# One backbone step: the first MLP product by seven products of blocks in place of eight

## The chip, the core and the metric

One Trainium2 chip, one core. A core has a matrix engine (TensorE, PE in the profile; PEld is its loading of weights), a vector engine (VectorE, DVE), a scalar engine (ScalarE, ACT), GpSimd (POOL), and SyncE (SP), whose queue issues nearly all DMA transfers here. Each runs its instructions in their written order and waits on semaphores for the others. Sixteen DMA engines move data between DRAM and on-chip memory. The metric is device time of one execution, in microseconds (us).

## What is computed

One inference step of a layer on 640 tokens (512 of a sample, 128 of a prompt) of width D = 1024: modulated normalisation, four token mixers (pooling, Fourier, RWKV-7, gated linear attention), a gated merge, an output product and a residual; then the part that is changed:

```
h  = rmsnorm(xf) * (1 + scale) + shift
ff = square(relu(h @ mlp_w1)) @ mlp_w2      # w1: 1024 x 4096, w2: 4096 x 1024
xf = xf + g2 * ff                           # then a last rmsnorm
```

All of it is fp32. TensorE's fast form (`fp32r`) keeps fewer bits, so each fp32 operand is split into a high part (a cast) and a low part (what the cast lost), and a product is three matmuls: high x high, low x high, high x low.

## The kernel before

It is recorded in Python through tile pools; a scheduler sets each engine's order, and work under `hi()` goes ahead of other work. Weights come through one helper: `fetch` (L241) has SP load a tile of 128 x 512 (256 KB) into one of three raw buffers `wr`; `split` has ACT cast it to the high part (L246) and DVE subtract for the low part (L247), after which the raw buffer is free.

Before the MLP, the output product (L1247) runs tile by tile of 128 tokens. For each tile, `projected` (L1307 to L1309) adds the residual to `xf` on DVE and has ACT sum the squares, `normed` makes the reciprocal root on DVE (`rs`, L1313 to L1316), and `transposed` has PE transpose the tile (L1332), ACT apply scale and shift into `tm` (L1336) and cast to `nh` (L1338), DVE subtract for `nl` (L1339). The last tile (i = 4) is transposed within the MLP's first group.

The MLP has four groups of 8 feature tiles of 128 (32 tiles make 4096). In a group the first product comes first: `hidden` (L1361) runs 24 matmuls (8 steps of 128 along D, three terms) for a feature tile and one half of the tokens (HN = 320), then ACT and DVE make relu squared and split it into `fh` and `fl` (L1365 to L1368). The second product (L1407, 512 columns wide) sums the 8 feature tiles into five PSUM banks for each half of the output columns, and `residual` (L1395, L1396) multiplies by g2 and adds to `xf`. The last half of the last group stands apart (L1427), so that each tile of tokens can be finished and stored.

In the RWKV scan, earlier on, `new_x` has POOL copy inputs of a step (L854), twice per step.

Of the kernel before, what the change touches and what calls it, by code (L numbers as in the profile page):

```python
# [19 lines left out]
P = 128  # L20
# [116 lines left out]
def backbone(ctx, tc, a, y_prompt, y_sample, out_rwkv, out_gla):  # L137
# [482 lines left out]
        finish()  # L620
    pf_.close()

    def split_into(y, j, src):
        S.copy(y[0][:, j, :], src)
        V.tensor_tensor(y[1][:, j, :], src, f32(y[0][:, j, :]), ALU.subtract)
# [60 lines left out]
    for hp in range(2):  # L686
# [161 lines left out]
        def new_x(step):  # L848

            x = upool.tile([P, 4, 2, 2, 64], F32, name="xc", tag="xc", bufs=3)  # L850
            for smp in (True, False)[: 2 if step < 2 else 1]:
                ch = slice(0, 2) if smp else slice(2, 4)
                for O_, par in ((HR[0], 1), (HR[1], 0)):
                    (S.copy if step == 0 else G.tensor_copy)(x[O_, ch, par], pick(VT, step, smp)[O_].unsqueeze(2).broadcast_to([64, 2, 2, 64]))  # L854
            return x

        x = new_x(0)
# [425 lines left out]
    nh = h2.tile([P, KT, NT], F32R, name="nh")  # L1283
    nl = h2.tile([P, KT, NT], F32R, name="nl")
    pf1 = ctx.enter_context(tc.tile_pool(name="pf1", bufs=3, space=PSUM, reuse_waits="tile"))
    ops = ExitStack()
    op = ops.enter_context(tc.tile_pool(name="opool", bufs=1, side="right", reuse_waits="tile"))

# [12 lines left out]
    def projected(i, hf, acc, t):  # L1301
        c = i // 4
        if c not in g1b:
            g1b[c] = h2.tile([P, D], F32, name="g1b", tag="g1b")
# [4 lines left out]
        S.activation(t[:, bs], xf[i][:, bs], AF.Square, accum_out=ss[:, 2 * i + hf : 2 * i + hf + 1])  # L1309

    def normed(i, t):
        with hi():
# [6 lines left out]
    def project(i, hfs, t):  # L1319
        for hf in hfs:  # L1320
# [2 lines left out]
                out_terms(acc, i, k, hf)  # L1323
            projected(i, hf, acc, t)

    def transposed(i, t):
        c = i // 4
        sl_ = slice(i * P, i * P + P)
        for k4 in range(2):
            pt = pbank()  # L1330
            for k in range(4):
                PE.transpose(pt[:, k * P : k * P + P], t[:, (k4 * 4 + k) * P : (k4 * 4 + k) * P + P], ident)  # L1332
            tm = op.tile([P, 4, P], F32, name="tm", tag="tm", bufs=2)
            for k in range(4):
                kk = k4 * 4 + k
                S.activation(tm[:, k], pt[:, k * P : k * P + P], AF.Identity, scale=s2[:, kk, c : c + 1], bias=b2[:, kk, c : c + 1])  # L1336
            ks = slice(k4 * 4, k4 * 4 + 4)
            S.copy(nh[:, ks, sl_], tm)  # L1338
            V.tensor_tensor(nl[:, ks, sl_], tm, f32(nh[:, ks, sl_]), ALU.subtract)  # L1339

    for i in range(4):
        projected(i, 0, accs[i], ot())
# [10 lines left out]

    with tc.tile_pool(name="mlp", bufs=1, reuse_waits="tile") as mp, \
            tc.tile_pool(name="pf2", bufs=5, space=PSUM, reuse_waits="tile") as pf2:
        def hidden(w, h, l, b):
            pt = pbank()
            bs = slice(b * HN, b * HN + HN)
            for k in range(KT):
                for n, (wk, m) in enumerate(((w[0], nh), (w[0], nl), (w[1], nh))):  # L1360
                    PE.matmul(pt[:, :HN], lhsT=wk[:, k, :], rhs=m[:, k, bs], start=k == 0 and n == 0,  # L1361
                              stop=k == KT - 1 and n == 2)
            with hi():
                rl = mp.tile([P, HN], F32, name="rl", tag="rl", bufs=3)
                S.activation(rl, pt[:, :HN], AF.Relu)  # L1365
                V.tensor_tensor(rl, rl, pt[:, :HN], ALU.mult)  # L1366
                S.copy(h[:, bs], rl)
                V.tensor_tensor(l[:, bs], rl, f32(h[:, bs]), ALU.subtract)  # L1368

        g2b = mp.tile([P, 2, D], F32, name="g2b")  # L1370
        gf = mp.tile([P, D], F32, name="gf")
        NG = 4
        for g in range(NG):
            ws, fh, fl = [], [], []
            order = [(f, b) for f in range(8) for b in range(2)]
            if g == 0:
                order[:4] = [(0, 0), (1, 0), (0, 1), (1, 1)]
            for f, b in order:
                if b == 0:
                    ws.append(load(a["t_w1"][g * 8 + f]))  # L1380
                    fh.append(mp.tile([P, NT], F32R, name="fh", tag="fh", bufs=11))
                    fl.append(mp.tile([P, NT], F32R, name="fl", tag="fl", bufs=11))
                elif f == 0 and g == 0:
                    with hi():
                        transposed(4, before)
                    ops.close()
                hidden(ws[f], fh[f], fl[f], b)
            if g == 0:
                for cnd in range(2):
                    nc.sync.dma_start(out=g2b[:, cnd, :], in_=grow[1][cnd : cnd + 1, :].broadcast_to([P, D]))  # L1390
                nc.sync.dma_start(out=gf, in_=a["final_g"].rearrange("(o d) -> o d", o=1).broadcast_to([P, D]))
            def residual(i, hf, acc):
                cs_ = slice(hf * 512, hf * 512 + 512)
                t = mp.tile([P, 512], F32, name="mt", tag="mt", bufs=3)
                V.tensor_tensor(t, g2b[:, i // 4, cs_], acc, ALU.mult)  # L1395
                V.tensor_tensor(xf[i][:, cs_], xf[i][:, cs_], t, ALU.add)  # L1396

            for hf in range(2 if g < NG - 1 else 1):
                acc = [pf2.tile([P, 512], F32, name="pf2", tag="pf2") for _ in range(5)]
                for k2 in range(4):  # L1400
                    wh, wl = load(a["t_w2"][g * 4 + k2, hf])
                    for kk in range(2):
                        k = k2 * 2 + kk
                        for i in range(5):
# [6 lines left out]
                        residual(i, hf, acc[i])  # L1411


        h2pool.close()
        with tc.tile_pool(name="w2pool", bufs=1, side="right", reuse_waits="tile") as w2p:
# [54 lines left out]
```

## Time and profile before

| what | value |
|---|---|
| median of 3 runs | 1220.24 us (1218.92 to 1222.08) |
| profiled execution | 1224.66 us, its span 1222.9 us |
| granted clock, mean | 0.988 |
| PE busy | 1176.4 us (96%) |
| DVE busy | 733.5 us (60%) |
| ACT busy | 506.7 us (41%) |
| POOL busy | 62.3 us (5%) |
| chain that ended last | PE 77%, DVE 8%, DMA 7%, ACT 4% |

The span goes from the first to the last instruction of the profiled execution; the rest of its time lies around it. The chain is followed back from the last instruction, each step to what released it. Rows of windows read: stretch in us, its length, then busy us and instructions (x) of PE, PEld, DVE, ACT and POOL, then the granted clock of PE as a share of full speed (1.00 is 2.4 GHz), the share of the DMA engines' time, and GB/s. In rows of a timeline the bracket tells how long the engine stood before, and what ended that.

### The profile page before, as it was taken

What the parts mean: (1) busy time and instruction counts of PE and PEld (TensorE: products, weight loads), DVE (VectorE), ACT (ScalarE), POOL (GpSimd) and SP (SyncE); (2) the same over time, 40 slices, a digit from 0 to 9 for tenths busy, and PEclk for the clock granted to TensorE, in tenths of its full rate; (3) what the DMA queues carried; (4) which work ended last, traced back from release to release, by engine and by line L of the source; (5) the groups of instructions that cost most, each with busy time, mean ns of one, the idle gap of its engine ahead of it and who ended that gap; (6) DMA issues with size and microseconds to landing.
All of it is one profiled execution on the core that took longest, in us unless ns stands there. A gap on an engine that the chain in (4) does not pass through costs nothing.

```text
span 1222.9 us, 19633 instructions
## 1 busy us (share of the span) xinstructions
PE 1176.4 (96%) x7556; PEld 1017.1 (83%) x7556; DVE 733.5 (60%) x1458; ACT 506.7 (41%) x1028; POOL 62.3 (5%) x98
## 2 busy tenths in 40 slices
PE   7999999899999999997999989999999999999996
PEld 2778998789778898795588978998899899889985
DVE  4797785675588583447987757543443354245456
ACT  4732225742376522378635325532143123213332
POOL 0000000500114200300000000000000000000000
PEclk9999898999999999999999999999999999999999
DMA  9558661334314343056624560322222222222222
GB/s 357 205 173 251 201 224 57 104 93 119 101 36 122 103 148 95 30 170 212 195 93 141 179 208 18 99 75 69 77 79 85 71 79 78 70 87 69 78 87 86
DMA packets 85971, 147.41 MB, mean 121 GB/s; under 512 B 21693, under 2 KB 26206, under 8 KB 85878
## 3 DMA queue, kind: packets, MB, share of 16 engines
q1 hardware_dynamic: 85878, 146.16, 37.8%
q8 instruction: 59, 0.97, 0.3%
q14 instruction: 34, 0.28, 0.1%
HBM read 123.17 MB, written 22.95 MB: 119 GB/s over the span
## 4 chain that ended last, share of the span: by engine, by line
PE 77%; DVE 8%; DMA 7%; ACT 4%; issue 3%; SPq 0%; POOL 0%; DVEq 0%; ACTq 0%; POOLq 0%
PE pt L368 23%; PE pf L1361 18%; PE pf L1407 16%; PE po L1247 3%; PE pf L1427 2%; PE px L1084 2%; DMA araw<-in_t_ada_dram 2%; PE px L499 2%; DVE acc L309 2%; DVE wl L247 1%; PE px L287 1%; DMA wr<-in_t_in_dram 1%; DMA wr<-in_t_out_dram 1%; DMA wr<-in_t_w_dram 1%; PE px L775 1%
## 5 line engine op out<-in xcount | busy, mean ns | idle before, releaser
L246 ACT CAST wh<-wr 128x512 fp32r<-128x512 f32 x222 | 133.4, 618 | 349.5 <-PE pf L1407 139.1
L247 DVE TENSOR_TENSOR wl<-wr,wh 128x512 fp32r<-128x512 f32 x222 | 152.2, 700 | 206.9 <-ACT wh L246 202.4
L368 PE MATMUL pt<-xl,wh 128*128 128x320 f32 x816 | 200.5, 321 | 0.0
L368 PE MATMUL pt<-xh,wh 128*128 128x320 f32 x816 | 199.7, 321 | 0.0
L368 PE MATMUL pt<-xh,wl 128*128 128x320 f32 x816 | 196.1, 318 | 0.0
L1361 PE MATMUL pf<-nh,wl 128*128 128x320 f32 x512 | 158.1, 309 | 0.0
L1361 PE MATMUL pf<-nl,wh 128*128 128x320 f32 x512 | 158.0, 309 | 0.0
L1361 PE MATMUL pf<-nh,wh 128*128 128x320 f32 x512 | 157.9, 309 | 0.0
L368 PEld LDWEIGHTS pt<-xh,wh 128*128 128x128 f32 x816 | 138.9, 191 | 8.8 <-issue 4.1
L368 PEld LDWEIGHTS pt<-xl,wh 128*128 128x128 f32 x816 | 139.5, 191 | 6.8 <-issue 3.0
L368 PEld LDWEIGHTS pt<-xh,wl 128*128 128x128 f32 x816 | 138.9, 191 | 4.9 <-issue 1.7
L1407 PE MATMUL pf<-wl,fh 128*128 128x512 f32 x280 | 109.0, 389 | 0.0
L1407 PE MATMUL pf<-wh,fh 128*128 128x512 f32 x280 | 109.0, 389 | 0.0
L1407 PE MATMUL pf<-wh,fl 128*128 128x512 f32 x280 | 108.9, 389 | 0.0
L1361 PEld LDWEIGHTS pf<-nl,wh 128*128 128x128 f32 x512 | 96.0, 187 | 0.2
L1361 PEld LDWEIGHTS pf<-nh,wh 128*128 128x128 f32 x512 | 96.0, 188 | 0.1
L1361 PEld LDWEIGHTS pf<-nh,wl 128*128 128x128 f32 x512 | 96.0, 187 | 0.0
L309 DVE SCALAR_TENSOR_TENSOR acc<-araw,sc,acc 128x512 f32<-128x512 f32 x112 | 78.4, 746 | 11.9 <-DMA araw<-in_t_ada_dram 11.9
L1407 PEld LDWEIGHTS pf<-wh,fl 128*128 128x128 f32 x280 | 52.6, 188 | 11.0
L1407 PEld LDWEIGHTS pf<-wh,fh 128*128 128x128 f32 x280 | 52.6, 188 | 10.9
L1407 PEld LDWEIGHTS pf<-wl,fh 128*128 128x128 f32 x280 | 52.6, 188 | 10.7
L1366 DVE TENSOR_TENSOR rl<-rl,pf 128x320 f32<-128x320 f32 x64 | 31.0, 484 | 39.0 <-ACT rl L1365 39.0
(540 smaller groups left out, 1754.2 us busy)
## 6 DMA issues: line engine op xcount, KB each, us to landing
wr<-in_t_w_dram SPq DMA_DIRECT2D x128, 256.0 KB, 3.0
wr<-in_t_in_dram SPq DMA_DIRECT2D x102, 256.0 KB, 3.5
araw<-in_t_ada_dram SPq DMA_DIRECT2D x64, 256.0 KB, 3.5
adaw<-in_t_ada_dram SPq DMA_DIRECT2D x16, 512.0 KB, 9.2
mscr<-gate SPq DMA_DIRECT2D x24, 320.0 KB, 4.3
mg<-mscr SPq DMA_DIRECT2D x24, 320.0 KB, 3.8
uscr<-mg SPq DMA_DIRECT2D x15, 320.0 KB, 2.8
wr<-in_t_branch_dram SPq DMA_DIRECT2D x32, 128.0 KB, 2.1
```

What stands on the lines that cost most here:

```text
L246: S.copy(wh, raw)
L247: V.tensor_tensor(wl, raw, f32(wh), ALU.subtract)
L287: PE.matmul(pt[0:8, :], lhsT=c[:, 4 * part : 4 * part + 8, k + j], rhs=w[:, j], start=part == 1 and k + j == 0 and n == 0, stop=part == 0 ...
L309: V.scalar_tensor_tensor(acc[j], raw, w, acc[j], ALU.mult, ALU.add)
L368: PE.matmul(pt[:, b, :HN], lhsT=w, rhs=m[:, b * HN : b * HN + HN], start=start and n == 0, stop=stop and n == 2)
L499: PE.matmul(pt[:, :HN], lhsT=lhsT, rhs=rhs[:, b * HN : b * HN + HN], start=True, stop=True)
L1084: PE.matmul(pt, lhsT=ek[:, ts_], rhs=em[:, :, ts_], start=True, stop=True)
L1247: PE.matmul(acc, lhsT=m[k][:, sl_], rhs=W[k, hf][w][:, 0, :], start=k == 0 and n == 0, stop=k == KT - 1 and n == 2)
L1361: PE.matmul(pt[:, :HN], lhsT=wk[:, k, :], rhs=m[:, k, bs], start=k == 0 and n == 0, stop=k == KT - 1 and n == 2)
L1366: V.tensor_tensor(rl, rl, pt[:, :HN], ALU.mult)
L1407: PE.matmul(acc[i], lhsT=m[k][:, ts_], rhs=w[:, kk, :], start=k == 0 and n == 0, stop=k == 7 and n == 2)
L1427: PE.matmul(acc, lhsT=m[k][:, ts_], rhs=ws[k][w][:, 0, :], start=k == 0 and n == 0, stop=k == 7 and n == 2)
```

## The change

The tokens are cut into two halves (t0, t1), D into two halves, and the feature tiles go in pairs, so that a pair is a product of 2 x 2 blocks (token half x half of D, times half of D x feature tile). That took eight block products; now seven make it, after a scheme with sums of blocks (Strassen's, in Winograd's form). A block product is 12 matmuls (4 steps along half of D, three terms) of 320 columns. Sums of activation blocks are made once, in `block_sums`; sums of weight blocks are made for each pair and kept in DRAM (`wsum`), for group 0 by eight DMAs of 1 MB on POOL's queue during the RWKV scan (four copies, then four that add), for groups 1 to 3 by loads, DVE adds and stores (`weight_sums`), recorded in the second product of the group before. The results of the seven products are combined on DVE as they come out of PSUM. `t_w1` is laid out anew on the host, in these blocks. Further, `nh` and `nl` hold only the first half of the tokens, `nf` keeps the normalised activations in fp32, `xf` is written to DRAM (`xres`) and its buffer used for the sum of the second product, and g2 and the residual are applied once, in the last group.

```diff
-        "t_w1": blocks(x["mlp_w1"][0], range(0, FF, P), P),
+        "t_w1": np.ascontiguousarray(blocks(x["mlp_w1"][0], range(0, FF, P), P).reshape(16, 2, P, 2, 512).transpose(3, 1, 0, 2, 4)),
...
+        def begin(n, g):
+            src = w1b[(0, 0, 1, 1)[n], (0, 1, 1, 0)[n], 4 * g : 4 * g + 4]
+            return lambda: nc.gpsimd.dma_start(out=rows(wsum[n][g]), in_=rows(src))
+        def add(n, g):
+            src = (w1b[0, 1, 4 * g : 4 * g + 4], w1b[1, 1, 4 * g : 4 * g + 4], wsum[0][g], wsum[2][g])[n]
+            return lambda: nc.gpsimd.dma_start(out=rows(wsum[n][g]), in_=rows(src), accum_op=ALU.add, max_dma_last_dim=8192)
+        return [begin(n, 0) for n in range(4)] + [add(n, 0) for n in range(4)]
...
+            if step > 0:
+                chore(1, last)
...
+    def block_sums(pool):
+        a11, a12, a21, a22 = nf[:, 0:4, t0], nf[:, 4:8, t0], nf[:, 0:4, t1], nf[:, 4:8, t1]
+        def put(name, s):
+            h, l = (pool.tile([P, 4, HN], F32R, name=f"{n}{name}") for n in ("sh", "sl"))
+            S.copy(h, s)
+            V.tensor_tensor(l, s, f32(h), ALU.subtract)
+            r[name] = (h, l)
+        put("22", a22)
+        V.tensor_tensor(a22, a22, a21, ALU.subtract)
+        put("22-21", a22)
+        V.tensor_tensor(a21, a11, a21, ALU.subtract)
+        V.scalar_tensor_tensor(a11, a22, -1.0, a11, ALU.mult, ALU.subtract)
+        put("21-22-11", a11)
+        put("11-21", a21)
+        V.scalar_tensor_tensor(a12, a11, -1.0, a12, ALU.mult, ALU.subtract)
+        put("22-21+11-12", a12)
...
+        def product(pt, m, src, first):
+            with hi():
+                wh, wl = load(src.unsqueeze(1), mp, "st", 4)
+                wh, wl = wh[:, 0], wl[:, 0]
+            mh_, ml_ = A[m]
+            for k in range(4):
+                ks = slice(k * P, k * P + P)
+                for n, (w, x) in enumerate(((wh, mh_), (wh, ml_), (wl, mh_))):
+                    PE.matmul(pt[:, :HN], lhsT=w[:, ks], rhs=x[:, k, :], start=first and k == 0 and n == 0,
+                              stop=k == 3 and n == 2, skip_group_check=True)
...
+        def first_pairs():
...
+            for j in range(2):
+                ba = bank(0)
+                product(ba, "11", w1b[0, 0, j], True)
+                p1.append(st())
+                with hi():
+                    S.copy(p1[j], ba)
+                product(ba, "12", w1b[1, 0, j], False)
...
+            yield
...
+                product(bd[j], "22", w(j, 3), True)
...
+                product(bc[j], "22-21", w(j, 0), True)
...
+                product(bb[j], "21-22-11", w(j, 2), True)
...
+        def pair_steps(j):
...
+            product(ba, "11", b11, True)
+            with hi():
+                S.copy(p1, ba)
+            yield
+            product(bb, "21-22-11", wsum[2][g][q], True)
+            with hi():
+                V.tensor_tensor(u2, p1, bb, ALU.add)
+            yield
+            product(ba, "12", b21, False)
...
+            product(bc, "22-21", wsum[0][g][q], True)
+            product(bb, "11-21", wsum[1][g][q], False)
...
+            product(bb, "22", wsum[3][g][q], False)
+            with hi():
+                V.tensor_tensor(p1, p1, bb, ALU.add)
+                V.scalar_tensor_tensor(p1, p1, 0.0, p1, ALU.max, ALU.mult)
+                parts_of(p1, h0, l0, t1)
+            yield
+            product(bc, "22-21+11-12", b22, False)
...
+                now = first_pairs()
+                next(now)
+                with hi():
+                    transposed(4, before)
...
+                    A.update(block_sums(spool.enter_context(tc.tile_pool(name="spool", bufs=1, reuse_waits="tile"))))
...
+            def weight_sums(g, q):
+                b11, b12, b21, b22 = (trp.tile([P, 512], F32, name="tr", tag="tr", bufs=4) for _ in range(4))
+                for t, (kh, fh_) in ((b11, (0, 0)), (b12, (0, 1)), (b22, (1, 1)), (b21, (1, 0))):
+                    nc.sync.dma_start(out=t, in_=w1b[kh, fh_, 4 * g + q])
+                for n, t, s in ((0, b11, b12), (1, b12, b22), (2, b22, b11), (3, b21, b22)):
+                    V.tensor_tensor(t, t, s, ALU.add)
+                    nc.sync.dma_start(out=wsum[n][g][q], in_=t)
...
                     wh, wl = load(a["t_w2"][g * 4 + k2, hf])
+                    if g < NG - 1 and k2 % 2 == 1:
+                        weight_sums(g + 1, hf * 2 + k2 // 2)
```

Where the instructions stand now, at three places. First DVE, from the normalisation of the last tile of tokens on (`ot` is that tile, `sh`/`sl` and `nf` of 128x1280 are the block sums, `stl` the low parts of weights). Before:

```order
L1316 TENSOR_SCALAR ot_7914<-xf4_7630,rs1_7999 128x512
L1366 TENSOR_TENSOR rl_8059<-rl_8059,pf1_8034 128x320
L1316 TENSOR_SCALAR ot_7914<-xf4_7630,rs1_7999 128x512
L1339 TENSOR_TENSOR nl_7635<-tm_7990,nh_7634 128x4x128
L1368 TENSOR_TENSOR fl_8033<-rl_8059,fh_8032 128x320
L1339 TENSOR_TENSOR nl_7635<-tm_8111,nh_7634 128x4x128
```

DVE in the changed kernel, from the same place:

```order
L1350 TENSOR_SCALAR ot_7945<-xf4_7654,rs1_8025 128x512
L247 TENSOR_TENSOR stl_8232<-wr_8233,sth_8231 128x512
L247 TENSOR_TENSOR stl_8251<-wr_8252,sth_8250 128x512
L1436 TENSOR_TENSOR fl_8051<-sums_8137,fh_8050 128x320
L1368 TENSOR_TENSOR sl22_8165<-nf_7671,sh22_8164 128x1280
L1372 TENSOR_TENSOR nf_7671<-nf_7671 128x4x320
L1374 TENSOR_TENSOR nf_7671<-nf_7671 128x4x320
L1368 TENSOR_TENSOR sl22-21_8170<-nf_7671,sh22-21_8169 128x1280
L247 TENSOR_TENSOR stl_8270<-wr_8271,sth_8269 128x512
L1375 SCALAR_TENSOR_TENSOR nf_7671<-nf_7671 128x4x320
L247 TENSOR_TENSOR stl_8291<-wr_8292,sth_8290 128x512
L247 TENSOR_TENSOR stl_8311<-wr_8312,sth_8310 128x512
```

In place of `nl` of 512 elements, five subtractions and four sums of 1280 stand between the weight splits. Second SP, which issues the loads; before, from the MLP's start to its end:

```order
L1305 DMA g1b<-grow_111 128x1024 x2
L1390 DMA g2b<-grow_112 128x1024 x2
L1391 DMA gf<-in_final_g_dram 128x1024
L241 DMA wr<-in_t_w_dram 128x512 x121
```

SP in the changed kernel, within the first product of group 1 (`tr` are blocks loaded for sums, `wsum_1` the sums that this group uses, `wsum_3` those of group 3):

```order
L1615 DMA wsum_3_1462<-tr 128x512
L241 DMA wr<-in_t_w_dram 128x512
L1615 DMA wsum_3_1466<-tr 128x512
L241 DMA wr<-wsum_1_1460 128x512
L1615 DMA wsum_3_1470<-tr 128x512
L241 DMA wr<-wsum_1_1464 128x512
L1615 DMA wsum_3_1474<-tr 128x512
L241 DMA wr<-in_t_w_dram 128x512
L1612 DMA tr<-in_t_w_dram 128x512
L241 DMA wr<-wsum_1_1472 128x512
L1612 DMA tr<-in_t_w_dram 128x512 x2
```

Loads and stores of sums stand between the loads of weights, in the first products of groups 0 (its second half) and 1 and in the second product of group 0; groups 2 and 3 have none. Third POOL, in the RWKV scan; before:

```order
L854 COPY xc<-VT 64x2x128 x16
L859 MEMSET xc 64x2x64 x2
L698 MEMSET TT 128x1280
```

POOL in the changed kernel, at the end of the same scan:

```order
L633 DMA wsum_0_1471<-in_t_w_dram 16x16384
L881 COPY xc<-VT 64x2x128 x2
L637 DMA wsum_0_1459<-in_t_w_dram 128x2048
L881 COPY xc<-VT 64x2x128 x2
L637 DMA wsum_0_1463<-in_t_w_dram 128x2048
L881 COPY xc<-VT 64x2x128 x2
L637 DMA wsum_0_1467<-wsum_0_1459 128x2048
L888 MEMSET xc 64x2x64 x2
L725 MEMSET TT 128x1280
```

Each DMA is issued behind a step's copies and ahead of the next step's; seven stand in the first scan, the eighth in the second.

## Rows read from the trace of the kernel before

**Rows 1.** The chain that ended last, 750 to 1223: start us, us, what
```profile
774.22 51.71 PE pf L1361 x352
825.93 54.47 PE pf L1407 x240
880.40 56.32 PE pf L1361 x384
936.72 54.44 PE pf L1407 x240
...
1158.24 27.24 PE pf L1407 x120
```

**Rows 2.** Busy us by engine in MLP windows; then PEclk, DMA share, GB/s
```profile
880.00:937.00 57.00, 57.00 (x388) 56.88 (x387) 27.56 (x53) 22.20 (x47) 0.00 (x0) 1.00 0.24 75
937.00:991.00 54.00, 54.00 (x240) 44.68 (x238) 19.78 (x33) 9.53 (x18) 0.00 (x0) 1.00 0.25 78
```

**Rows 3.** Groups by line and form, 774 to 1185: busy us, mean ns
```profile
L247 DVE TENSOR_TENSOR wl<-wr,wh 128x512 fp32r<-128x512 f32 x116 | 77.9, 688 | 158.8 <-ACT wh L246 158.8
L246 ACT CAST wh<-wr 128x512 fp32r<-128x512 f32 x116 | 69.1, 617 | 198.7 <-PE pf L1407 139.1 <-PE pf L1361 59.7
...
L1368 DVE TENSOR_TENSOR fl<-rl,fh 128x320 fp32r<-128x320 f32 x64 | 31.5, 492 | 14.2 <-ACT fh L1367 14.2
L1366 DVE TENSOR_TENSOR rl<-rl,pf 128x320 f32<-128x320 f32 x63 | 30.5, 484 | 39.0 <-ACT rl L1365 39.0
L1367 ACT CAST fh<-rl 128x320 fp32r<-128x320 f32 x63 | 29.0, 460 | 26.6 <-DVE rl L1366 26.6
```

**Rows 4.** Timeline, all engines, turn into the MLP: start us, us
```profile
767.25 0.69 DVE L1307 TENSOR_TENSOR ot<-g1b,po 128x512 f32<-128x512 f32 x1 [4.03 <-PE po L1247]
...
767.84 0.39 PE L1361 MATMUL pf<-nh,wh 128*128 128x320 f32 x1
...
769.49 0.16 DVE L1313 TENSOR_TENSOR ss<-ss 128x1 f32<-128x1 f32 x1 [0.82 <-ACT ot L1309]
...
772.08 0.49 DVE L1316 TENSOR_SCALAR ot<-xf,rs 128x512 f32<-128x512 f32 x1
...
772.71 0.63 PE L1332 MATMUL pf<-cst,ot 128*128 128x128 f32 x4 [0.37 <-ACT nh L1338]
...
773.38 1.86 ACT L1336 ACTIVATE tm<-pf,b,s 128x128 f32<-128x128 f32 x5
```

**Rows 5.** Timeline of PE around two pauses: [idle before <-releaser]
```profile
650.44 0.83 PE L368 MATMUL pt<-yh,bh 128*128 128x320 f32 x2 [2.02 <-ACT yh L624]
...
731.55 0.50 PE L1247 MATMUL po<-wo01h,mh 128*128 128x512 f32 x1 [1.48 <-DVE ot L1307]
```

**Rows 6.** Windows behind these two pauses, columns as before
```profile
650.00:651.00 1.00, 0.56 (x2) 0.43 (x2) 0.94 (x2) 1.00 (x3) 0.00 (x0) 0.77 0.00 0
651.00:652.00 1.00, 0.97 (x5) 0.70 (x4) 0.61 (x2) 1.00 (x2) 0.00 (x0) 0.50 0.00 0
652.00:654.00 2.00, 2.00 (x9) 2.00 (x9) 1.06 (x2) 0.64 (x2) 0.00 (x0) 0.51 0.00 0
654.00:658.00 4.00, 4.00 (x29) 4.00 (x28) 2.41 (x4) 0.63 (x2) 0.00 (x0) 1.00 0.21 66
733.00:740.00 7.00, 7.00 (x32) 5.77 (x32) 4.47 (x9) 3.19 (x10) 0.00 (x0) 1.00 0.00 0
```

**Rows 7.** DMA issues, 880 to 937: KB each, us to landing
```profile
wr<-in_t_w_dram SPq DMA_DIRECT2D x16, 256.0 KB, 3.0
```

**Rows 8.** Windows of heavy loading, columns as before
```profile
8.00:28.00 20.00, 20.00 (x42) 5.28 (x42) 10.41 (x25) 11.89 (x19) 0.00 (x0) 1.00 1.03 409
96.00:124.00 28.00, 25.34 (x161) 22.90 (x159) 21.35 (x35) 8.01 (x14) 0.00 (x0) 1.00 0.83 262
```

**Rows 9.** Timeline of POOL in the RWKV scan, 318 to 372
```profile
325.34 1.34 POOL L854 COPY xc<-VT 64x256 f32<-64x256 f32 x2 [3.58 <-PE pxc L909]
...
349.93 0.45 POOL L859 MEMSET xc<- 64x128 f32 x2 [4.37 <-PE pxc L909]
```

More of the change, by code (lines that the diff above doesn't have):

```diff
@@ L621, in backbone, with sum_steps, rows, chore @@
     pf_.close()
+    wsum = [[dpool.tile([4, P, 512], F32, name=f"wsum{n}_{g}") for g in range(4)] for n in range(4)]
+    w1b = a["t_w1"]
+    def sum_steps():
+        def rows(t):
+            return t.rearrange("j p c -> (j p) c")
+        def begin(n, g):
[5 more added lines that the diff above has]
+        return [begin(n, 0) for n in range(4)] + [add(n, 0) for n in range(4)]
+    chores = sum_steps()
+    def chore(n, ins):
+        with tc.issue_after(ins.ins):
+            for _ in range(min(n, len(chores))):
+                chores.pop(0)()
     def split_into(y, j, src):
@@ L853, in new_x @@
                 for O_, par in ((HR[0], 1), (HR[1], 0)):
-                    (S.copy if step == 0 else G.tensor_copy)(x[O_, ch, par], pick(VT, step, smp)[O_].unsqueeze(2).broadcast_to([64, 2, 2, 64]))
+                    last = (S.copy if step == 0 else G.tensor_copy)(x[O_, ch, par], pick(VT, step, smp)[O_].unsqueeze(2).broadcast_to([64, 2, 2, 64]))
+            if step > 0:
+                chore(1, last)
             return x
@@ L1282, in backbone @@
     h2 = h2pool.enter_context(tc.tile_pool(name="h2pool", bufs=1, side="right", reuse_waits="tile"))
-    nh = h2.tile([P, KT, NT], F32R, name="nh")
-    nl = h2.tile([P, KT, NT], F32R, name="nl")
+    nh = h2.tile([P, KT, HN], F32R, name="nh")
+    nl = h2.tile([P, KT, HN], F32R, name="nl")
+    xres = [dpool.tile([P, D], F32, name=f"xres{i}") for i in range(5)]
     pf1 = ctx.enter_context(tc.tile_pool(name="pf1", bufs=3, space=PSUM, reuse_waits="tile"))
+    nfs = ExitStack()
+    nf = nfs.enter_context(tc.tile_pool(name="nfpool", bufs=1, side="right", reuse_waits="tile")).tile([P, KT, NT], F32, name="nf")
     ops = ExitStack()
@@ L1303, in projected @@
         if c not in g1b:
-            g1b[c] = h2.tile([P, D], F32, name="g1b", tag="g1b")
+            g1b[c] = op.tile([P, D], F32, name="g1b", tag="g1b")
             nc.sync.dma_start(out=g1b[c], in_=grow[0][c : c + 1, :].broadcast_to([P, D]))
@@ L1309, in projected @@
         S.activation(t[:, bs], xf[i][:, bs], AF.Square, accum_out=ss[:, 2 * i + hf : 2 * i + hf + 1])
+        if hf == 1:
+            nc.sync.dma_start(out=xres[i], in_=xf[i])
     def normed(i, t):
@@ L1355, in backbone @@
             tc.tile_pool(name="pf2", bufs=5, space=PSUM, reuse_waits="tile") as pf2:
[L1356 to L1362, printed above, removed]
-            with hi():
[L1364 to L1368, printed above, removed]
@@ L1372, in backbone @@
         NG = 4
         for g in range(NG):
-            ws, fh, fl = [], [], []
-            order = [(f, b) for f in range(8) for b in range(2)]
+            fh, fl = [], []
+            before_ = None
             if g == 0:
[L1377 to L1385, printed above, removed]
-                    ops.close()
-                hidden(ws[f], fh[f], fl[f], b)
@@ L1388, in backbone @@
-            if g == 0:
+                now = first_pairs()
+                next(now)
+                with hi():
+                    transposed(4, before)
+                    ops.close()
+                    A.update(block_sums(spool.enter_context(tc.tile_pool(name="spool", bufs=1, reuse_waits="tile"))))
+                nfs.close()
+                trs = ExitStack()
+                trp = trs.enter_context(tc.tile_pool(name="trpool", bufs=1, side="right", reuse_waits="tile"))
+                for _ in now:
+                    pass
@@ new lines, in backbone @@
+            for j in range(0 if g else 2, 4):
+                now = pair_steps(4 * g + j)
+                next(now)
+                if before_:
+                    next(before_)
+                next(now)
+                if before_:
+                    next(before_)
+                next(now)
+                before_ = now
+            next(before_)
+            next(before_)
+            if g == NG - 1:
+                spool.close()
+                trs.close()
+                h2pool.close()
+                w2pool = ExitStack()
+                w2p = w2pool.enter_context(tc.tile_pool(name="w2pool", bufs=1, side="right", reuse_waits="tile"))
+                g2b = w2p.tile([P, 2, D], F32, name="g2b")
+                gf = w2p.tile([P, D], F32, name="gf")
@@ L1411, in backbone @@
                         residual(i, hf, acc[i])
-        h2pool.close()
-        with tc.tile_pool(name="w2pool", bufs=1, side="right", reuse_waits="tile") as w2p:
+        with w2pool:
             ws = [load(a["t_w2"][(NG - 1) * 4 + k // 2, 1, :, k % 2 : k % 2 + 1], w2p, f"w2{k}", 1) for k in range(8)]
```

106 lines of the change are left out of this document (98 added, 8 removed).

## The prediction

> **What bounds the kernel now.** I read the chain of waits first, over the last third of the span. From 774.22 on it is TensorE alone: 384 matmuls of the first product in 56.32 us (146.7 ns each), then 240 of the second in 54.4 us (226.8 ns), four times over [rows 1]. The windows of one group say the same from the other side: PE is busy for the whole stretch at granted clock 1.00, while DVE has 27.56 of 57 us to do, ACT 22.20, and the DMA engines are at a share of 0.24 [rows 2]. So here a matmul taken away is time taken away, until another engine or the weight stream ends last. The rows by line give the price of what such an engine gets to do [rows 3], and the timeline of the turn into the MLP shows how little PE stands there now: the first MLP matmul starts at 767.84, and one stall of 0.37 us follows [rows 4].
>
> **Part 1: the matmuls.** Eight block products of 12 matmuls for a pair of feature tiles become seven: 336 for 384 per group, 192 fewer in all. Width and form stay, so 192 x 146.7 ns = **-28.2 us**, 7.0 per group. This holds only where PE stays fed.
>
> **Part 2: the turn into the MLP (group 0).** The order of PE puts only four products (with "11" and "12") ahead of those that need the sums of activations. These sums are a chain: last tile of tokens transposed, ACT writes it to `nf`, ACT casts 128x1280, DVE subtracts, DVE makes the next sum, and again. No row shows an op of 1280. From the forms of 320 and 512, ACT grows by 157 ns for 192 elements and DVE by 196 [rows 3], so I estimate 1.25 us for a cast and 1.5 for a DVE op. I laid the new orders of the three engines over the times of before [rows 4]:
> - The first product waits for a weight subtraction that now stands behind the multiplication at 767.25: 0.6 us. "12" waits twice for ACT to copy "11" out of PSUM: about 0.5 and 1.3.
> - The normalisation of the last tile keeps its length (769.49 to 772.08), but runs later and between weight splits, so its transposes come at about 776 and 777, and PE is through with the four products at 778.1.
> - ACT needs eight writes to `nf` of 0.37 (five in 1.86) beside its work on "12"; the cast for "22" ends at 782.7, its subtraction at 784.2. PE stands for 4.6 us, then 1.4. (24 matmuls of "22" last 3.5.)
> - Two sums and a subtraction later "22-21" is ready at 788.6 (PE stands 1.0). Until "21-22-11" is ready at 795.4, DVE has three more wide ops and four splits to do: PE stands 3.3.
>
> That is 12.7 us of standing, against 0.9 in before (767.84 to 825.93 is 58.1 for 56.3 of matmuls and 0.9 of transposes): **+11.8**. No later than 795 the chain is worked off, and nothing else in this group waits on it.
>
> **Part 3: the clock.** These pauses may cost more than their length. After a pause of 2.02 us at 650.44 [rows 5] the granted clock went to 0.77, 0.50 and 0.51 up to 654, then back to 1.00 [rows 6]: about 3.3 us at 1.2 GHz for 2.4, half of it lost, 1.6 us. After one of 1.48 at 731.55 [rows 5] it stayed at 1.00 [rows 6]. Here there are two pauses of more than 3 us. Bounds: 0, if work that waits anyway lies in the slow stretch, and 7, if each costs twice what that one did. I take **+3.5**.
>
> **Part 4: feeding PE in the other groups.** A weight tile of 256 KB now serves 12 matmuls (1.76 us) for 24 (3.52). Landing takes 3.0 us [rows 7], cast 0.62 and subtraction 0.69 [rows 3]: 4.3 us for a raw buffer, of which three make 5.3 us. That is enough, with 1 us to spare and four split tiles ahead. DVE in a group: 28 splits (19.3 us), seven ops from sums or PSUM per pair (4 x 7 x 0.484 = 13.6), four `fl` per pair (7.9): 40.7 of 49.3 us. ACT: 28 x 0.617 and 36 of 0.46, 33.9. So groups 2 and 3, which have no sums in them, keep their 7 us; for a queue that is closer to its need I take +0.5 each (0 to 4): **+1**. The second product loses one DVE op per tile of output, which was hidden; the ten wide ops and five loads that return in group 3 lie beside 27 us of PE work: 0.
>
> **Part 5: the sums of weights.** Twelve sets of four loads, four DVE adds and four stores must run between about 806 us (pairs 2 and 3 of group 0) and the end of the first product of group 1: 96 transfers. With 14, 16 and 28 weight tiles in this stretch that is 154 x 0.262 MB = 40.4 MB in 24.6 + 54.4 + 49.3 = 128.3 us, or 315 GB/s, where before had 75 to 78 [rows 2]. The heaviest windows of the trace are bounds: 409 GB/s with a deep queue of 512 KB loads (8 to 28 us), and 262 GB/s at a share of 0.83 where loads of 256 KB are mixed with others, as here (96 to 124) [rows 8]. At 409 the stretch needs 99 us, so nothing is lost; at 262 it needs 154: 26 us lost. SP issues all of it in one order, and a store that waits for its add holds the weight loads behind it; in group 1 the 16 adds (16 x 0.688 = 11.0) also bring DVE to 51.7 us by durations for PE's 49.3. I take 300 GB/s, above the lower row, since there other queues' data set when SP could issue, and below the upper one, where all loads stood ready: 134.7 us, **+6** (0 to 26). What DVE lacks in group 1, 2.4 us, lies within it.
>
> **Part 6: DMAs on POOL during the RWKV scan.** Eight of 1 MB, one after a step's copies. POOL sits 3.58 to 4.37 us idle before its next op there, waiting for PE [rows 9], so an issue is hidden if it takes less. Nothing shows its length; the nearest row is a POOL op itself, a pair of copies in 1.34. Bounds 0 to 8 (1 us past cover in each); I take **+1**.
>
> **Sum.** -28.2 + 11.8 + 3.5 + 1 + 6 + 1 = -4.9 on the profiled execution of 1224.66: 1219.8. The median of the runs, 1220.24, is 4.4 below that execution, so I carry the difference over: 1215.3, said as **1215**.
>
> **Rivals.**
> *A. PE is fed all along.* The queue does overlap as in 8 to 28 us, and the clock holds as at 731.55. For it: no engine is over its time in groups 2 and 3; against it: SP's single order. Only part 2 and 1 us remain: -28.2 + 11.8 + 1 = -15.4, about **1205**.
> *B. The traffic of the sums ends last* (slower than before). Place: second product of group 0 and first product of group 1; PE waits for weights behind stores on SP. Price: at 262 GB/s +26 for my +6, which gives 1235; at 280 GB/s 144 us, +16: **1225**. It decides from where the stretch of 128 us takes over 15 us more, that is below about 282 GB/s. For it: the row of 96 to 124 has the same kind of load and the same SP order; against: the row of 8 to 28.
> *C. The gain is eaten evenly.* The raw buffers become the bound: if landing grows from 3.0 to 4.1 us under twice the traffic, a buffer takes 5.4 us, 1.80 per tile for 1.76; 28 tiles in each of three groups give +3.4 for my +1, and both pauses at their full clock price +7 for my +3.5: about **1221**, no change. For it speaks how little the three buffers have to spare, against it the four split tiles that PE has ahead.
> *D. POOL's DMAs hold the scan.* A pair of POOL's copies takes 1.34 there already, so little is left of 3.58 once an issue comes on top. If each issue outlasts its cover by 1 us, +7 more: **1222**.
>
> The Trainium skill speaks for D: its page "SBUF — State Buffer", section "SBUF: two separate sides", says that a DMA issued from GpSimd has its descriptors written by that engine, which is locked out while DVE runs an op in a two-port mode. By that rule the eight DMAs would start late, and POOL's next copies behind them; no run here shows such a DMA yet.
>
> **How the numbers follow.** My forecast has 0.40, with its own range 1208 to 1220; A 0.20 (1202 to 1208); B 0.25 (1222 to 1236); C 0.10; D 0.05. A measurement of this kernel tells 0.3% (3.7 us) from no change: faster is below 1216.6, slower above 1223.9. Faster: 0.28 of the forecast, A's 0.20, 0.03 of C and 0.01 of D; slower: 0.21 of B, 0.02 of C and 0.02 of D; the rest, 0.23 (0.12 of it the forecast's), is no change. For 8 in 10 the range goes from 1203 to 1229: the lower edge leaves out a fifth of A, the upper what B costs below 273 GB/s.
>
> **What would show it.** In the changed profile PE should stand for some 12 us between 767 and 802, released by ACT and DVE lines of the block sums, with a granted clock of 0.5 just behind. Group 0's first product should end at about 830 plus the clock's cost, and the first products of groups 2 and 3 should last 49.3 us each without gaps. In the second product of group 0 and the first of group 1, PE's waits should name `wl` or `stl`, and add up to about 6 us, with 250 to 320 GB/s. Wrong would be: no standing at the turn (then ACT and DVE pass my order by), first products of groups 2 and 3 over 51 us (then C), over 15 us of waiting for weights around the sums (B), or a later start of the MLP than 767 (D).

## The result: no gain, by the medians 0.1 to 0.7% slower

| set of runs | before, median us | changed, median us | ratio, 95% interval |
|---|---|---|---|
| first | 1221.16 (4 runs) | 1231.13 (1226.38 to 1232.68, 4 runs) | 1.0068 [1.0039, 1.0097] |
| second | 1221.35 (29) | 1223.04 (1214.03 to 1231.36, 12) | 1.0009 [0.9979, 1.0039] |
| third | 1224.27 (17) | 1230.50 (1224.25 to 1236.29, 12) | 1.0048 [1.0025, 1.0071] |

The forecast was 1215, in a range of 1203 to 1229. The medians of the first and third sets lie above that range; only the second is within it (its ratio can't be told from 1), and no set shows a gain. Single executions of either kernel scatter by some 15 us, so the sets differ; what follows rests on medians of one set, on ratios to the kernel before, and on stretches within one profile.

The profile of the changed kernel is of its fastest run of the first set (1226.38). On its page PE has less to do, and DVE and ACT more:

```profile
span 1224.4 us, 19820 instructions
## 1 busy us (share of the span) xinstructions
PE 1152.1 (94%) x7364; PEld 989.1 (81%) x7364; DVE 812.8 (66%) x1577; ACT 548.7 (45%) x1103; POOL 66.8 (5%) x106
```

PE is busy 24.3 us less, yet the span is as long. The chain shows where it went. Groups 2 and 3 look as they should (the answer to [rows 1]; start us, us, what):

```profile
887.03 5.44 DMA wsum<-tr
892.48 2.03 DMA tr<-in_t_w_dram
894.51 0.70 DVE tr L1614
...
951.21 53.06 PE pf L1628 x234
1004.27 45.71 PE pf L1428 x312
```

From 951 to 1158 the chain is PE alone, 146.5 ns for a matmul as before. In group 1, just ahead, it runs through stores and loads of the weight sums and DVE's adds. The windows (answer to [rows 2]; same columns) say it by stage: the turn into the MLP, then the second product of group 0 with the first of group 1, then the next two stages:

```profile
770.00:790.00 20.00, 13.80 (x75) 12.18 (x73) 15.00 (x21) 14.65 (x27) 0.00 (x0) 0.83 0.33 97
790.00:800.00 10.00, 7.71 (x52) 7.72 (x53) 9.05 (x14) 3.92 (x6) 0.00 (x0) 1.00 0.38 120
823.00:951.00 128.00, 114.88 (x613) 102.10 (x612) 79.34 (x142) 50.86 (x100) 0.00 (x0) 0.97 0.84 276
951.00:1004.00 53.00, 53.00 (x236) 43.90 (x235) 18.57 (x31) 10.27 (x18) 0.00 (x0) 1.00 0.28 89
1004.00:1050.00 46.00, 46.00 (x315) 45.96 (x314) 33.74 (x63) 27.26 (x57) 0.00 (x0) 1.00 0.47 135
```

Between 823 and 951 PE stands for 13 us and runs a part of the rest below full clock (0.97 over the stretch), while the DMA engines are at a share of 0.84 and 276 GB/s. PE's own timeline names what it waited for, at the turn and then in group 1 (the bracket is the standing time):

```profile
779.00 0.90 PE L1428 MATMUL pf<-sh,sth 128*128 128x320 f32 x2 [4.45 <-ACT sh L1367]
780.53 0.63 PE L1428 MATMUL pf<-sl,sth 128*128 128x320 f32 x1 [0.63 <-DVE sl L1368]
792.29 0.41 PE L1428 MATMUL pf<-sl21-22-11_8176,sth 128*128 128x320 f32 x1 [2.41 <-DVE sl21-22-11_8176 L1368]
...
897.70 0.64 PE L1428 MATMUL pf<-sh11-21_8179,sth 128*128 128x320 f32 x1 [3.85 <-DVE sums L1520]
904.92 0.38 PE L1428 MATMUL pf<-sh,sth 128*128 128x320 f32 x1 [0.73 <-DVE sums L1531]
```

The releaser at 897.70 is an addition out of PSUM (L1520) of a product that was complete before PE stopped at 893.85. DVE's timeline shows why it was late:

```profile
893.78 2.87 DVE L1614 TENSOR_TENSOR tr<-tr 128x512 f32<-128x512 f32 x4 [7.15 <-DMA tr<-in_t_w_dram]
896.57 0.69 DVE L247 TENSOR_TENSOR stl<-wr,sth 128x512 fp32r<-128x512 f32 x1
897.17 0.48 DVE L1520 TENSOR_TENSOR sums<-sums,pf 128x320 f32<-128x320 f32 x1
```

For 7.15 us an add of weights stood at the head of DVE's queue and waited for its load. Landing times in the stretch answer to [rows 7] (KB each, us to landing):

```profile
wsum<-tr SPq DMA_DIRECT2D x44, 256.0 KB, 3.3
tr<-in_t_w_dram SPq DMA_DIRECT2D x42, 256.0 KB, 4.6
wr<-in_t_w_dram SPq DMA_DIRECT2D x33, 256.0 KB, 4.2
wr<-wsum SPq DMA_DIRECT2D x16, 256.0 KB, 3.8
```

A weight tile takes 4.2 us for 3.0. To measure a kernel by stages, take the stretch S from the first matmul of the MLP to the end of group 1's first product (where the chain passes to the second): 168.9 us before (767.84 to 936.72), 186.9 in the changed kernel (764.31 to 951.21). From there to the end of group 3's first product it is 221.5 before and 207.2 now: 14.3 us gained there, 18.0 lost in S. (The MLP began 3.5 us earlier in this profile, and from 1158 on it takes some 2 us longer; so the spans differ by only 1.5.)

### The profile page after: what moved, and what is told of

The parts are those of the page before. It is cut to its first block, busy times and chain, and to the rows that moved or that the text cites. A ratio compares the mean times of both kernels' runs of the same rounds, so it can differ in the third digit from the quotient of the medians.

```text
span 1224.4 us, 19820 instructions
## 1 busy us (share of the span) xinstructions
PE 1152.1 (94%) x7364; PEld 989.1 (81%) x7364; DVE 812.8 (66%) x1577; ACT 548.7 (45%) x1103; POOL 66.8 (5%) x106
## 4 chain that ended last, share of the span: by engine, by line
PE 59%; DMA 16%; DVE 14%; ACT 7%; issue 4%; SPq 1%; POOL 0%; DVEq 0%; ACTq 0%; POOLq 0%
PE pt L368 22%; PE pf L1428 10%; PE pf L1628 9%; PE po L1276 3%; DMA araw<-in_t_ada_dram 2%; DMA wr<-in_t_w_dram 2%; DMA tr<-in_t_w_dram 2%; DVE acc L309 2%; DVE wl L247 2%; PE px L499 2%; PE pf L1647 2%; DMA wsum<-tr 2%; DMA wr<-wsum 2%; DMA wr<-in_t_out_dram 2%; DMA wr<-in_t_in_dram 1%
## 5 line engine op out<-in xcount | busy, mean ns | idle before, releaser
L246 ACT CAST wh<-wr 128x512 fp32r<-128x512 f32 x158 | 95.0, 619 | 238.2 <-PE pt L368 110.9
L247 DVE TENSOR_TENSOR wl<-wr,wh 128x512 fp32r<-128x512 f32 x158 | 108.6, 704 | 94.2 <-ACT wh L246 89.5
L246 ACT CAST sth<-wr 128x512 fp32r<-128x512 f32 x112 | 69.1, 619 | 94.7 <-PE pf L1428 43.8
L247 DVE TENSOR_TENSOR stl<-wr,sth 128x512 fp32r<-128x512 f32 x112 | 76.9, 690 | 39.0 <-ACT sth L246 37.9
L1628 PEld LDWEIGHTS pf<-wh,fl 128*128 128x128 f32 x280 | 52.6, 188 | 10.7
L1614 DVE TENSOR_TENSOR tr<-tr 128x512 f32<-128x512 f32 x48 | 33.1, 689 | 32.5 <-DMA tr<-in_t_w_dram 32.2
L1435 ACT CAST fh<-sums 128x320 fp32r<-128x320 f32 x64 | 29.3, 459 | 27.1 <-DVE sums L1547 14.9
L1428 PE MATMUL pf<-nh,sth 128*128 128x320 f32 x128 | 40.4, 315 | 1.0 <-ACT sums L1463 0.9
L1428 PE MATMUL pf<-nh,stl 128*128 128x320 f32 x128 | 40.1, 313 | 0.2 <-DVE stl L247 0.2
L1428 PE MATMUL pf<-nl,sth 128*128 128x320 f32 x128 | 40.1, 313 | 0.0
```

Source lines behind the costliest of these rows:

```text
L246: S.copy(wh, raw)
L247: V.tensor_tensor(wl, raw, f32(wh), ALU.subtract)
L1428: PE.matmul(pt[:, :HN], lhsT=w[:, ks], rhs=x[:, k, :], start=first and k == 0 and n == 0, stop=k == 3 and n == 2, skip_group_check=True)
L1435: S.copy(h[:, bs], x)
L1614: V.tensor_tensor(t, t, s, ALU.add)
L1628: PE.matmul(acc[i], lhsT=m[k][:, ts_], rhs=w[:, kk, :], start=k == 0 and n == 0, stop=k == 7 and n == 2)
```

## Experiments

Theory S: the sums of weights (their 25 MB, or the order in which they are issued) keep PE waiting. Theory T: the turn into the MLP, with its chain of block sums and the slow clock, takes the gain. Theory P: the DMAs on POOL delay the scan. Each experiment changes one thing of the changed kernel, except the spread, which changes place, order and buffers together; the last two build on the one ahead of them. Small transfers, POOL's queue, the spread and the four pairs ran in one set with the kernel before (1222.84) but without the changed kernel; there the ratio to the kernel before is what compares (1.0009 to 1.0068 for the changed kernel).

**The changed kernel again**, in two sets, no edit.

> The changed kernel once more, as the base of this set. Its profiled execution (1226.38 us) was the fastest of four (up to 1232.68). Both theories expect a median of 1228 to 1232, and in the profile again some 180 to 190 us from the first matmul of the MLP to the end of group 1's first product (186.9 then, 168.9 before the change), while groups 2 and 3 keep their 7 us each.

> The changed kernel a third time: its first ratio to the kernel before was 1.0068 [1.0039, 1.0097] from four runs, the second 1.0009 [0.9979, 1.0039] from twelve. If the change is slower by over 0.3%, the ratio here is above 1.003; if it makes no difference that can be told, it is between 0.998 and 1.003.

Ratios 1.0009 and 1.0048, S = 185.8 and 186.4 us in their profiles: the loss in S repeats within 1.1 us. The first median, 1223.04, missed the 1228 to 1232 expected of it; the second ratio is above the 1.003 that was to mean slower, though its interval begins at 1.0025. Where the scatter comes from isn't settled: the profiled executions lie within 3 us of one another. The MLP began at 764 to 770 us in the profiles of kernels that do the same up to there, and the mean granted clock goes with the time (0.988 in the fastest execution of the first of these sets, 1214.03 us, 0.977 in the slowest, 1231.36).

**No sums of weights for groups 1 to 3.**

```diff
-                    if g < NG - 1 and k2 % 2 == 1:
-                        weight_sums(g + 1, hf * 2 + k2 // 2)
...
-            product(bc, "22-21", wsum[0][g][q], True)
+            product(bc, "22-21", wsum[0][0][q], True)
```

> Leaves out the sums of weights of groups 1 to 3 (loads, DVE adds, stores); these groups read group 0's sums instead. Theory S (the sums' transfers and adds keep PE waiting in group 0's second and group 1's first product): all pauses of PE behind 824 us and the clock's fall near 897 go, 16 to 20 us less: about 1212. Rival T (the turn into the MLP, with its chain of block sums and the slow clock behind it, is what eats the gain): these pauses only move elsewhere, 5 us less at most: 1225 or more.

1206.89 us, 16.2 below the base of its set; S = 168.8. Theory S holds, at the lower end of its price by the medians (16.2 for 16 to 20). PE no longer stands behind 823 us, while the turn is unchanged:

```profile
770.00:790.00 20.00, 13.64 (x76) 12.41 (x75) 14.36 (x23) 14.23 (x29) 0.00 (x0) 0.83 0.37 112
...
823.00:934.00 111.00, 110.87 (x622) 100.78 (x621) 54.47 (x99) 50.09 (x100) 0.00 (x0) 1.00 0.37 116
```

S is now what it was before the change, although 96 matmuls (14.1 us) fewer lie in it: the turn takes the other 14.

**The traffic without the adds.**

```diff
-                    V.tensor_tensor(t, t, s, ALU.add)
                     nc.sync.dma_start(out=wsum[n][g][q], in_=t)
```

> Leaves out only the 48 DVE adds of the sums; their loads and stores stay, a store follows its load. Theory S1 (an add that waits for its load stands at the head of DVE's queue, and the PSUM sums and weight splits behind it wait too): the pauses released by DVE sums go (13 us with the clock), 1218 to 1221. Theory S2 (the traffic itself and SP's single order delay the weight tiles): little changes, 1227 or more.

1224.33 us for 1223.04, S = 187.6: nothing is won. The time lies between the two ranges expected, which were worked out from a base of some 1230; but the 10 us or so that S1 promised did not come, so S1 falls. DVE has 57 us to do in the stretch for 79, and PE stands as long: 10.7 us here (119.3 of 130 busy), 9.6 to 13.1 in the changed kernel's three profiles. In its longest pause (7.1 us up to 910.07) DVE waited for a cast, and ACT for a weight tile:

```profile
908.19 0.62 ACT L246 CAST sth<-wr 128x512 fp32r<-128x512 f32 x1 [8.61 <-DMA wr<-wsum]
```

```profile
823.00:953.00 130.00, 119.33 (x653) 107.52 (x652) 57.09 (x106) 52.27 (x105) 0.00 (x0) 0.97 0.84 275
```

Here what stood at the head of DVE's queue was the place where the wait showed, not its cause. The DMA share and rate are those of the changed kernel.

**All transfers and adds, a sixteenth of the bytes** (reading as in the run without sums).

```diff
-                    nc.sync.dma_start(out=t, in_=w1b[kh, fh_, 4 * g + q])
+                    nc.sync.dma_start(out=t[:, :32], in_=w1b[kh, fh_, 4 * g + q][:, :32])
...
-                    nc.sync.dma_start(out=wsum[n][g][q], in_=t)
+                    nc.sync.dma_start(out=wsum[n][g][q][:, :32], in_=t[:, :32])
```

> Keeps every transfer and add of the weight sums and their order, but of 32 columns for 512 (a sixteenth of the bytes); groups 1 to 3 read group 0's sums. Theory B (bytes: 40 MB in this stretch at the 275 to 290 GB/s that the DMA engines then move, share 0.85): nearly all of the 16 us comes back, about 1208. Theory O (order: SP stands for a store whose add is not done, or for a buffer not stored yet, with weight loads behind): no more than 5 us come back, 1218 or more.

1208.19 us, ratio 0.9881 [0.9846, 0.9916], against 0.9883 for the run without sums; S = 171.1 for 168.8: theory B. The same number of transfers and adds in nearly the same order costs some 2 us once the bytes are gone.

```profile
823.00:938.00 115.00, 114.91 (x648) 104.60 (x647) 64.35 (x150) 51.66 (x104) 0.00 (x0) 1.00 0.48 129
```

This does not wholly part bytes from order, since a small transfer also lands sooner (2.2 us, for 3.3 and 4.6) and so shortens every wait behind it. SP's own waits for sums (what it waited for: us in total, times, longest), in the changed kernel between 823 and 951, then here between 823 and 938:

```profile
SPq L1615 <- DVE tr L1614: 27.5, 34, 2.6
SPq L1612 <- DMA wsum<-tr: 8.8, 7, 2.8
```

```profile
SPq L1615 <- DVE tr L1614: 10.1, 15, 2.0
SPq L1612 <- DMA wsum<-tr: 5.9, 6, 1.1
```

With full transfers SP stood 36.3 us behind adds and stores of sums, with loads of weights behind them in its order, while the DMA engines were busy for 0.84 of the time. The next run takes that order away.

**The sums' transfers on POOL's queue.**

```diff
-                    nc.sync.dma_start(out=t, in_=w1b[kh, fh_, 4 * g + q])
+                    nc.gpsimd.dma_start(out=t, in_=w1b[kh, fh_, 4 * g + q])
...
-                    nc.sync.dma_start(out=wsum[n][g][q], in_=t)
+                    nc.gpsimd.dma_start(out=wsum[n][g][q], in_=t)
```

> Moves the 96 transfers of the weight sums from SP's queue to POOL's; bytes and DVE adds stay. Theory O: weight loads no longer stand behind sums, 10 us less or more, 1213 or below. Theory B: the bytes still share the 16 DMA engines, 1219 to 1226. The one mixed case: POOL's own issue takes longer than SP's (0.5 to 0.85 us for one of its 1 MB DMAs against 0.33 to 0.42).

1247.71 us, ratio 1.0214 [1.0187, 1.0242], S = 205.7: worse than either theory said. With SP free of sums, weights still came late, and POOL, in its own order, stood for DVE's adds and for buffers (engine, what it waited for: us in total, times, longest):

```profile
POOL wsum L1615 <- DVE tr L1614: 50.6, 29, 4.5
DVE tr L1614 <- DMA tr<-in_t_w_dram: 30.9, 11, 6.6
POOL tr L1612 <- DMA wsum<-tr: 27.6, 18, 4.7
ACT sth L246 <- DMA wr<-in_t_w_dram: 23.8, 9, 11.7
```

So the order on SP alone is not the cause; that order and bytes act together is not excluded. The Trainium skill, "DMA: Bandwidth & Descriptors", section "Issuing engines are not separate DMA queues", says that transfers of all issuing engines run on the same 16 DMA engines; the run agrees (weight tiles land in 5.4 us here, 4.2 with all of it on SP). Why it is worse and not equal (18 to 25 us by the ratios, 19 to 20 in S) isn't settled: an issue takes 0.54 us on POOL, and the clock was lower (0.90 over the stretch).

**No DMAs on POOL** (group 0 reads unsummed blocks).

```diff
             if step > 0:
-                chore(1, last)
```

> Leaves out the eight DMAs on POOL; group 0 reads unsummed blocks instead. Theory P (1 MB DMAs fill the 16 DMA engines in the RWKV scan, so that a load of the token shift on SP's queue lands late, 13 us for 3 to 4, and DVE and PE stand behind it): 4 to 5 us less, about 1226. Rival: POOL's DMAs are hidden and the difference before the MLP is chance of the run: within 1 us of the base.

1220.10 for 1223.04: between the two expectations, and the intervals overlap, so the times settle nothing. The mechanism shows in the first profile of the changed kernel, in the scan:

```profile
322.04 0.82 DVE L699 TENSOR_TENSOR ut<-ut 128x638 f32<-128x638 f32 x1 [3.54 <-DMA ut<-uscr]
...
323.33 0.64 PE L964 MATMUL pxc<-p,TT 64*64 64x64 f32 x8 [3.72 <-DVE ut L701]
```

The load that DVE waits for is on SP's queue. It took 13.0 us for 320 KB here, 4.2 in the kernel before and 3.8 in this run, where that wait is gone. In the third profile the load took 6.9 us, and DVE waited 2.7 and PE 2.9 us. In the second profile, that of this set's base, it took 7.0 us and nothing waited; the same line has no standing time in front of it:

```profile
323.26 1.01 DVE L699 TENSOR_TENSOR ut<-ut 128x638 f32<-128x638 f32 x1
```

So POOL's transfers slow this load in all three profiles and cost PE up to 3.7 us, in two of them; the delay is in the load's landing, and no row shows POOL itself late.

**No block sums of activations** (every product reads the first block).

```diff
-                    A.update(block_sums(spool.enter_context(tc.tile_pool(name="spool", bufs=1, reuse_waits="tile"))))
+                    A.update({m: A["11"] for m in ("22", "22-21", "21-22-11", "11-21", "22-21+11-12")})
```

> The changed kernel without block sums of activations: every product reads the first block of the first half of the tokens, so PE waits for no chain of casts and subtractions at the turn into the MLP; matmuls, weights and weight sums stay. Theory T (the chain costs 12 to 14 us with the clock): the pauses of 4.4, 0.6 and 2.4 us there go and the clock stays at 1.00 up to 800; since group 0 then ends earlier, the weight sums press more, and 3 to 5 us come back as waits for weights: 8 to 11 us less than the base, 1212 to 1215. Rival: all of it comes back as waits for weights: 1220 or more.

1212.66 us, 17.8 below the base of its set; S = 173.8, 12.6 below. Both are more than the 8 to 11 expected; that the time fell into 1212 to 1215 is luck, as that range came from a base of 1223 and this set's is 1230.50. The long pauses at the turn are gone, at full clock:

```profile
764.00:800.00 36.00, 33.87 (x214) 31.44 (x213) 23.25 (x50) 22.73 (x52) 0.00 (x0) 1.00 0.62 199
```

So T is true beside S. Against the bases of their sets, taking out the weight sums gave 17.0 us of S, and taking out the block sums 12.6.

**Sums spread over the three second products.** Loads, adds and stores get edges of order: four loads behind the weight loads of an even step, adds a step later, stores two steps later; eight buffers for four.

```diff
+            def sums_loaded(g, q):
+                with tc.issue_after(last["dma"].ins):
+                    ts = [trp.tile([P, 512], F32, name="tr", tag="tr", bufs=8) for _ in range(4)]
...
+            def sums_added(ts):
+                b11, b12, b22, b21 = ts
+                with tc.issue_after(last["sub"].ins):
...
+                        if k2 % 2 == 0:
+                            if q:
+                                sums_stored(g + 1, q - 1, ts_q)
+                            ts_q = sums_loaded(g + 1, q)
+                        else:
+                            sums_added(ts_q)
```

> The sums of group g+1 stay inside the second product of group g: four loads behind the weight loads of an even step, adds one step later behind the last weight split, stores two steps later; eight buffers for four. The same bytes are spread over three second products (231 GB/s in each) in place of 315 over one stretch. Theories B and O both expect 10 to 15 us less than the base's 1223: 1208 to 1213, with all pauses behind 824 us below 1 us each. If instead the transfers only take their cost with them, all three groups lose 5 us: 1222.

1213.08 us, ratio 0.9925 [0.9900, 0.9950] to the kernel before: 10 us below it, as expected. S = 171.7, no pause of PE between 824 and 1157 is over 0.6 us, and the second products run gap-free with the same bytes:

```profile
837.00:891.00 54.00, 54.00 (x240) 44.58 (x240) 23.88 (x40) 15.58 (x29) 0.00 (x0) 1.00 0.68 224
942.00:995.00 53.00, 53.00 (x235) 43.89 (x234) 28.65 (x47) 10.19 (x18) 0.00 (x0) 1.00 0.69 228
```

**Four pairs' first products ahead of the block sums**, on top of the last edit.

```diff
-            for j in range(2):
+            for j in range(4):
                 ba = bank(0)
                 product(ba, "11", w1b[0, 0, j], True)
...
+            for js in ((0, 1), (2, 3)):
```

> As the run before this one, and in group 0 the products 11 and 12 of all four pairs come before those that need block sums, which gives PE 7 us of work during the chain of casts and subtractions. In the profiles of the change PE stood 8.6 us there and ran 5 us long at a clock of 0.7 to 0.9. Theory T (the turn costs 12 to 14 us in all, of which the clock is a third): 8 to 11 us less than the run before. Rival: DVE and ACT, with more splits among the wide operations, finish the chain as much later: 3 us less at most.

1208.32 us, ratio 0.9880 [0.9847, 0.9914]. By the medians that is 4.8 less, half of what theory T expected, but the two intervals overlap, and S = 170.0 is only 1.7 below; that is within the rival's 3 us. The long pause shrinks from 4.4 to 0.7 us, but "22-21" now waits 2.3 us, and the clock falls there in place of 770 to 790 (0.83 over 780 to 800; the "0.7 to 0.9" of the expectation is such a mean, the low level itself is 0.50):

```profile
780.00:800.00 20.00, 14.90 (x75) 13.72 (x75) 15.47 (x16) 11.52 (x20) 0.00 (x0) 0.83 0.27 80
```

**POOL's DMAs in the second scan**, on top of both edits.

```diff
-            if step > 0:
-                chore(1, last)
+            if step > 0 and hp == 1:
+                chore(2 if step == 1 else 1, last)
```

> As the run with four pairs first, and the eight DMAs on POOL all stand in the second RWKV scan, where the profile before shows the DMA engines at a share of 0.15 to 0.18 between 480 and 520 us. Theory P (in the first scan they delay a load of the token shift and PE stands about 4 us): 3 to 4 us less, about 1205. Rival: other loads of the second scan are delayed as much: no difference from 1208.

1204.28 us, ratio 0.9829 [0.9802, 0.9857]: the best of all, 20 us below the kernel before. Against the run without this edit it is 4 us by the medians; they come from different sets and the intervals of the ratios overlap, and in the two profiles the MLP begins no earlier (765.0 for 764.3; S = 167.9 for 170.0). So only the wait's going is shown (no wait for `ut` in the first scan, 2.9 us in the run ahead, and 80.00 of 80 us busy on PE in the second):

```profile
440.00:520.00 80.00, 80.00 (x869) 67.91 (x868) 35.13 (x89) 24.41 (x61) 15.02 (x21) 1.00 0.63 158
```

## Why the prediction was wrong, step by step

| part | forecast, us | measured, us | from |
|---|---|---|---|
| 1 matmuls | -28.2 | -28.2 | 146.5 ns each; 14.3 of 14.1 in groups 2 and 3 |
| 2 and 3, turn and clock | +15.3 | +13 to 14 | S without sums, S without block sums |
| 4 feeding | +1 | 0 | 207.2 for 221.5 less 14.1 |
| 5 sums of weights | +6 | +16 to 18 | run without sums: medians and S |
| 6 POOL | +1 | 0 to +4 | PE's wait behind `ut`, three profiles |
| tail | 0 | +2 | 57.2 for 55.3 from 1158 on |
| sum | -4.9 | +3 to +10 | |

The medians of the three sets lie 10.0, 1.7 and 6.2 us above the kernel before.

**Part 5 failed by its size**: +6 was forecast, +16 to 18 measured, which is most of the miss. Its mechanism and place were those foreseen, its price that of rival B (+16), which had a chance of 0.25 where the forecast had 0.40. I took 300 GB/s for the stretch because I put the row of 96 to 124 down to other queues' data, and looked for a value between two rows. The stretch made 276 GB/s in the first profile, 281 in the third, at a share of 0.84 to 0.85: nearly the lower row (262 at 0.83, there 18 loads of 256 KB with 4 stores of 320 KB among others). 409 GB/s was loads alone, all ready, and not of 512 KB only: 12 of these and 4 of 256 KB [rows 8]. A demand of 315 GB/s was above what the trace had shown for this kind, and nothing but the deep-queue row spoke for more. PE stood 13.1 us between 823 and 951 for the 6 expected, which is short of the 15 that were to mean B; and 7.9 of it name PSUM sums on DVE, not `wl` or `stl`, since the wait for a weight shows at what stands behind it.

**Parts 2 and 3** were right in their sum. The pauses were 8.6 us for the 12.7 worked out ("22-21" didn't wait, the copies out of PSUM cost 0.9 in one place). The clock cost at most 3.4 us in the first profile (0.83 over 20 us; PE stood in a part of the slow time, which costs nothing more), and in the run with small transfers at most 6.9 (0.74 over 770 to 790, 0.83 over 790 to 800). As in [rows 5, 6] it fell at a long pause, here within the one that ended at 779.00, and was 0.50 up to about 784:

```profile
777.00:779.00 2.00, 0.00 (x0) 0.00 (x1) 0.14 (x2) 1.92 (x3) 0.00 (x0) 0.60 0.44 131
779.00:784.00 5.00, 4.37 (x15) 3.97 (x16) 4.93 (x4) 1.66 (x2) 0.00 (x0) 0.50 0.00 0
```

The length of a pause alone doesn't tell it, as [rows 5, 6] may suggest: the pause of 2.41 us at 792.29 left the clock at 1.00 (790 to 800), and in the third profile one of 1.78 us was followed by 0.51:

```profile
877.40 0.50 PE L1628 MATMUL pf<-wl,fh 128*128 128x512 f32 x1 [1.78 <-DVE wl L247]
878.00:881.00 3.00, 3.00 (x9) 2.35 (x8) 0.55 (x1) 0.00 (x0) 0.00 (x0) 0.51 0.78 266
```

**Part 4** held, and so did its margin of 1 us: groups 2 and 3 show no pause. What I costed at nothing in group 3 was not hidden: ten wide DVE ops came back there, and PE stood up to 1.7 us for `mt` behind them.

**Part 6** had the right sign where it cost anything, and the wrong path. Rival D spoke of POOL's issue. An issue took 0.49 to 0.85 us there, and POOL's copies were not late by themselves; the sign named for D, a start of the MLP later than 767, did not come (764.3). As to the rule that went with D (the Trainium skill, "SBUF — State Buffer", section "SBUF: two separate sides"): no row shows the issue held up; whether a part of the 10 us that such a DMA took to land is due to it, no run here tells.

**The carried difference** added to the miss: I took 4.4 us off because the profiled execution was above the median, but the changed kernel's profiled executions lie 4.8 below, 2.7 above and 2.0 below the medians of their sets, so such a difference does not carry over.

## What to carry to other kernels

Before adding traffic to a stretch, divide its bytes by the stretch's length and compare with what the trace shows for the same kind of transfer; over that rate, expect the excess as time, whichever engine the waits then name. Here the forecast's 40.4 MB at the 276 GB/s that the stretch made give an estimate of 146 us for 128, 18 more, and 16 to 18 were lost. The scheduler had pulled the sums of three groups into one stretch; edges of order that kept them in the stretches with room, consumers a step behind producers, and more buffers won 10 us together. Removing matmuls from a PE-bound stage paid here only where the work that replaced them started early enough; a pause at the turn cost its length and the slow clock behind it.

## What the runs showed of the hardware

- 16 DMA engines moved 275 to 281 GB/s at a share of 0.84 to 0.85 with 256 KB loads and stores mixed, against 409 at 1.03 with loads alone (12 of 512 KB, 4 of 256). Whether the mixed rate would rise without SP's waits, no run shows.
- A few 1 MB transfers between DRAM and DRAM on POOL's queue (medians of 6.7 to 11.6 us to land) went with 13.0, 7.0 and 6.9 us for a 320 KB load on SP's queue in three profiles, for 4.2 and 3.8 without them.
- The granted clock went to 1.2 GHz at PE's pauses of 1.78, 2.02 and 4.45 us, and stayed at 2.4 behind pauses of 1.48 and 2.41 us, all in otherwise busy stretches.
- The same 96 transfers cost 18 to 25 us more on POOL's queue than on SP's (ratio 1.0214 for 1.0009 to 1.0068).
